# Gate columns and mLSTM values of a hybrid transformer block as one token-major product, done within the projections of another head group

## The chip, the cores and the metric

The kernel runs on one core of one Trainium2 chip. The metric is the device time of the whole program in microseconds (us): the median of three runs. All times are in us unless marked ns.

## The reference

Two layers work on 256 context tokens and 512 latent tokens of width 1024, in float32. Each layer norms and modulates the tokens, multiplies them with one input matrix whose columns belong to four groups of heads, joins what the groups give, multiplies with an output matrix, and then runs a gated MLP. Cut to what matters here:

```python
zx = split_cols(hx @ w_in)      # GDN q,k,v,z,a,b | SWA q,k,v | gMLP u,v | mLSTM q,k,v,o,i,f
a_x, a_c = gdn_mixer(...)       # bidirectional gated delta rule, chunks of 64 tokens
b_x, b_c = swa_mixer(...)       # windowed attention
c_x = gmlp_mixer(u, v, ...)     # u * (w_s @ rmsnorm(gelu(v)) + b_s), chunks of 128
d_x, d_c = mlstm_mixer(...)     # bidirectional mLSTM, chunks of 64
x = x + mod_x[2] * (concat(a, b, c, d) @ w_out)
x = x + mod_x[5] * mlp(...)
```

The gates of GDN (a, b) and of the mLSTM (i, f) are 16 columns each. They go through a softplus (GDN's decay and the mLSTM's forget gate); the mLSTM also needs a running maximum over all tokens.

## The kernel before, in words

Products run on TensorE in a split form: each float32 operand is split into a high part (ScalarE, `act_`, L182) and the rest (VectorE, L185 or L188), and three products are added: hi x hi, hi x lo, lo x hi (L179). The 768 tokens are one stretch of 256 (context) and one of 512 (latent); a projection of 128 columns (`gemm`) is 8 parts of the depth x 2 stretches x 3 products, 48 matmuls, with the weights stationary and the tokens streaming, and needs two PSUM buffers of the pool `pps` (four buffers, `ps()`). In the second layer some projections need the latent tokens alone. `gemm_pair` does two such projections in step, one part of the depth after the other, so that TensorE can begin while the norm's results `hhi` and `hlo` are still being made. `gemm_tok` does it the other way round: tokens stationary, 256 columns streaming, so that the result has tokens on its partitions; its results are called `mmt`, two blocks of 128 tokens to a PSUM buffer. `wload` loads 128 columns of weights (SP's queue, two buffers `wst`) and splits them into `whi` and `wlo`.

In one layer, `flow_kernel` goes in this order. (1) The pair behind the norm: the 32 gate columns, L620 and L632, and the first 128 columns of GDN's keys. The gates are copied out, transposed to tokens (`gatesT`, L636) and go through the softplus (L639 to L660), a chain of some 24 small VectorE operations that ends in `y` and `sp`. (2) The five other GDN projections, in the order v, k, v, q, q (L682 to L711), each followed by a convolution over tokens (four VectorE operations of 770 columns), a SiLU and, for k and q, a norm. (3) GDN's chunk work (L718 to L999): six steps of `gdn_pre`, `gdn_inv`, `gdn_kt` and `gdn_scan`, many small matmuls that wait for each other by way of VectorE and ScalarE. `N` is the first matrix of a chunk, `ops` the last matmuls of a step. Its tiles are in a pool `gd` that is closed at L1000 (`pa.close()`). (4) Projections of the other groups: attention (L1018 to L1030), the gMLP's values `vt` (L1058, `gemm_tok`) with their gelu (one buffer `tc`) and norm (L1067 to L1076), the mLSTM's keys and queries (L1087 to L1093), and the gMLP's mixing product `sg` (L1096 to L1110), the last reader of `vt`. (5) The mLSTM's gate scan (L1113 to L1198): cumulated sums `mb`, transposes `aRp`, the maximum scans (L1164) and what is made of them, `MD` last, in tiles of `tc`, `ta`, `tb` and a pool `sw1` opened behind `pa.close()` (`La`, `khi`). (6) The mLSTM's values, `va` (L1201 to L1204, `gemm_tok`, 144 matmuls). (7) A block `mix` (L1500 on) with attention, the mLSTM's chunks and the last projections woven together; its first matmuls are `decp`. Then come the output product and the MLP.

The order of the code is a priority: each engine gets the earliest instruction in the code that can go, so projections of stage (4) run in the gaps of stage (3). Buffers of one tag go to their users in the order of the code: `tc` has one, `ta` and `tb` two, the pool `pps` four, and `gi` and `go` one PSUM buffer each. The block `mix` begins only behind what stands before it on each engine.

Of the kernel before, what the change touches and what calls it, by code (L numbers as in the profile page):

```python
# [9 lines left out]
F32 = mybir.dt.float32  # L10
# [130 lines left out]
def flow_kernel(ctx, tc, t, out, dbg=None, stop=None):  # L141
# [20 lines left out]
    def ps(name="ps", dt=F32):  # L162
        return pps.tile([128, 512], dt, tag="ps", name=name)
# [20 lines left out]
    def tt(o, a, b, op, eng=None):  # L184
        (eng or V).tensor_tensor(out=o, in0=a, in1=b, op=op)  # L185
# [15 lines left out]
    def cc(name):  # L201
        o, w = _OFF[name]
        return cst[:, o:o + w]
# [75 lines left out]
    def evac(dst, o, segs, rows=128):  # L279
        for c0, cn in segs:  # L280
            act_(dst[:, c0:c0 + cn], o[bank(c0)][0:rows, 0:cn], AF.Copy)
# [196 lines left out]
    def wload(parts, order=None):  # L478
        st = wst.tile([128, 8, 128], F32, tag="wst", name="wst")
        o = 0  # L480
        for src in parts:
            n = src.shape[1]
            sv = src.rearrange("(k p) n -> p k n", p=128)
            for i in (range(0, 8, 2) if order else (0,)):
                if order:
                    nc.sync.dma_start(out=st[:, i:i + 2, o:o + n], in_=sv[:, order[i]:order[i] + 2])
                else:
                    nc.sync.dma_start(out=st[:, :, o:o + n], in_=sv)
            o += n
        return wsplit(st, o)  # L490
# [106 lines left out]
    for l in range(DEPTH):  # L597
# [19 lines left out]
        def z3(name, dt=F32):  # L617
            return zp.tile([128, NT], dt, tag="z3", name=name, bufs=6)

        ahead = [wload([win[:, C_AB:C_AB + 16], win[:, C_IF:C_IF + 16]]), wload([win[:, C_GK:C_GK + 128]])]  # L620
        h = modulated(l, 0, ALL, nrm, tp)
        del nrm
        xd = dp.tile([8, 128, NT], F32, tag="xd", name="xd")
# [3 lines left out]
        def temp(tag, w=GAP + 4):  # L627
            return tp.tile([128, GAP + 4], F32, tag=tag, name=tag, bufs=1 if tag == "tc" else 2)


        zg = temp("ta")
        o, o_k0 = gemm_pair(ahead, h, ALL, (32, 128))  # L632
        evac(zg[0:32], o, ALL, 32)
        o = ps("gatesT")
        for p in range(NP):
            T.transpose(o[:, 32 * p:32 * p + 32], zg[0:32, 128 * p:128 * p + 128], ident[0:32, 0:32])  # L636
        wb = z3("wb")
        ysp = z3("ysp")[:, 0:384].rearrange("p (x s g) -> p x s g", x=2, s=6)
        y, sp = ysp[:, 0], ysp[:, 1]  # L639
        u = temp("tb")[:, 0:192].rearrange("p (s g) -> p s g", g=32)  # L640
        w = temp("tc")[:, 0:192].rearrange("p (s g) -> p s g", g=32)
        tt(y, o[:, 0:192].rearrange("p (s g) -> p s g", g=32), bc(tokp[l][:, 0:32], 1, 6), ADD)
        tt(y, y, bc(cc("sgn"), 1, 6), MUL)
        nega = tokp[l][:, 32:40]
        act_(nega, nega, AF.Exp)
        V.tensor_scalar(out=nega, in0=nega, scalar1=-1.0, scalar2=None, op0=MUL)

        V.tensor_scalar(out=sp, in0=y, scalar1=-1.0, scalar2=None, op0=MUL)
        tt(u, sp, y, MAX)
        act_(u, u, AF.Exp, scale=-1.0)  # L650
        V.tensor_scalar(out=w, in0=u, scalar1=2.0, scalar2=None, op0=ADD)
        V.reciprocal(out=w, in_=w)
        tt(u, u, w, MUL)
        tt(w, u, u, MUL)
        V.tensor_scalar(out=sp, in0=w, scalar1=1.0 / 15, scalar2=None, op0=MUL)
        for cf in (13, 11, 9, 7, 5, 3):
            stt(sp, sp, 1.0 / cf, w, ADD, MUL)
        stt(sp, sp, 1.0, u, ADD, MUL)
        V.tensor_scalar(out=u, in0=y, scalar1=0.0, scalar2=None, op0=MAX)
        stt(sp, sp, 2.0, u, MUL, ADD)  # L660


        kq = [gd.tile([128, 2, GAP], F32, name=f"kq{j}") for j in range(2)]
# [16 lines left out]
                stt(x[:, a0:], x[:, a0:], f, e[:, a0:], MUL, MUL)  # L680

        cols = [(C_GK, C_GQ, C_GV)[which] + 128 * j for which, j in ((0, 0), (2, 0), (0, 1), (2, 1), (1, 0), (1, 1))]  # L682
        ready = {}
        for i, (which, j) in enumerate(((0, 0), (2, 0), (0, 1), (2, 1), (1, 0), (1, 1))):
            qlat = which == 1 and last
            segs = LAT if qlat else ALL
            o = gemm(None, h, segs, w2=ready.pop(i)) if i else o_k0
            if i < 5:
                ready[i + 1] = wload([win[:, cols[i + 1]:cols[i + 1] + 128]])
            raw = temp("ta")  # L690
            G.memset(raw[:, 0:2], 0.0)
            G.memset(raw[:, 258:260], 0.0)
            G.memset(raw[:, 772:774], 0.0)
            if not qlat:
                act_(raw[:, 2:258], o[0][:, 0:256], AF.Copy)
            act_(raw[:, 260:772], o[1], AF.Copy)
            a0 = 258 if qlat else 0
            acc = vf[j] if which == 2 else kq[j][:, which]
            cw = R_CONV + {0: 2, 1: 0, 2: 4}[which] + j
            act_(acc[:, a0:], raw[:, a0:GAP], AF.Copy, scale=prm[l][:, cw:cw + 1])  # L700
            for tp_ in range(1, 5):
                stt(acc[:, a0:], raw[:, a0 + tp_:GAP + tp_], prm[l][:, cw + 6 * tp_:cw + 6 * tp_ + 1], acc[:, a0:], MUL, ADD)
            e = temp("tb")[:, 0:GAP] if i % 2 else gd.tile([128, 1024], F32, tag="at", name="e", bufs=2)[:, 0:GAP]
            sigmoid_(acc[:, a0:], e[:, a0:])
            tt(acc[:, a0:], acc[:, a0:], e[:, a0:], MUL)
            if len(unit) > 2 - 1:
                unit_rows()
            if which < 2:
                act_(e[:, a0:], acc[:, a0:], AF.Square)
                unit.append((acc, e, a0, 0.125 if which else None))  # L710
# [344 lines left out]
            act_(w_, w_, AF.Exp, scale=-1.0)  # L1055
            tt(x, x, w_, MUL)

        vt = zp.tile([128, 6, 264], F32, tag="big", name="vt")[:, :, 0:256]  # L1058
        gemm_tok(l, C_MV, opairs, h, lambda p, o: act_(vt[:, p], o, AF.Copy))
        for p0, pn in ((0, 4), (4, 2)):  # L1060
            o = ps("svT")
# [34 lines left out]
        for j in range(2):  # L1096
            for p0 in range(opairs[0], NP, 4):
                pn = min(4, NP - p0)
                o = ps("sg")
                for p in range(p0, p0 + pn):  # L1100
                    for g in (2 * j, 2 * j + 1):
                        gp_ = slice(64 * (g % 2), 64 * (g % 2) + 64)
                        mm(o[gp_, 128 * (p - p0):128 * (p - p0) + 128], vt[:, p, 64 * g:64 * g + 64], wsT[:, g, :])
                n_ = 128 * pn
                mv = mix[4 + j][:, 128 * p0:128 * p0 + n_]
                sgt = temp("ta")[:, 0:n_] if early else mv
                stt(sgt.rearrange("p (a b) -> p a b", b=128), o[:, 0:n_].rearrange("p (a b) -> p a b", b=128),
                    prm[l][:, R_GMW + j:R_GMW + j + 1], bc(bsb[:, j], 1, pn), MUL, ADD)
                if early:
                    tt(mv, mv, sgt, MUL)  # L1110


        pb = ctx.enter_context(ExitStack())  # L1113
# [81 lines left out]
        for p in range(NP):  # L1195
            mm(o[:, 64 * p:64 * p + 64], bc(mlast[:, p], 1, 128), ident[0:64, 0:64])
        tt(ks, am, o[:, 0:384].rearrange("p (a d r) -> p a d r", a=6, d=2)[:, :, :, 0:4], SUB)
        act_(ks, ks, AF.Exp)  # L1198


        va = zp.tile([128, 6, 4, 66], F32, tag="big", name="va")  # L1201
        G.memset(va[:, :, :, 64:66], 1.0)
        gemm_tok(l, C_LV, list(range(NP)), h,
                 lambda p, o: act_(va[:, p, :, 0:64], o.rearrange("p (h i) -> p h i", h=4), AF.Copy))  # L1204

        if stop == "A":
            return
# [416 lines left out]
```

## Time and profile before

| | us |
|---|---|
| median of 3 runs | 1977.71 |
| lowest and highest run | 1973.69, 1981.29 |
| profiled execution, its own time | 1960.3 |
| its span, first to last instruction | 1958.5 |
| TensorE busy, share of the span | 96% |
| VectorE busy, share of the span | 61% |
| ScalarE busy, share of the span | 39% |
| mean granted TensorE clock | 0.979 |

The profile is of one execution. PE is TensorE, DVE is VectorE, ACT is ScalarE, POOL is GpSimd, SP issues most loads. Matmuls are pipelined, so the time from one to the next is shorter than one's duration. A row "out<-in" names the tile written and the tiles read; a bracket at the end of a row gives how long the engine had been idle before and what let it go.

### The profile page before, as it was taken

The page shows a single profiled execution, that of the slowest core. Times are in us where ns is not written, and L with a number is a line of the kernel's source. Part 1 is how long each engine was busy: PE and PEld are TensorE (multiplying, and loading weights), DVE is VectorE, ACT ScalarE, POOL GpSimd, SP SyncE. Part 2 cuts the span into 40 slices and gives each one's busy share as a digit, 9 for nine tenths or more (in the row PEclk, how much of TensorE's full clock was granted, in tenths as well). Part 3 has the DMA queues.
Part 4 walks back from the last instruction along what each step waited for, and adds up shares of the span by engine and source line. Part 5 has one row for each costly group of instructions (what it writes and reads, how often), then busy time and mean ns, then how long its engine had stood idle before and what let it go on. Part 6 is the DMA issues. An engine that isn't in the chain of part 4 may idle for free.

```text
span 1958.5 us, 33935 instructions
## 1 busy us (share of the span) xinstructions
PE 1881.4 (96%) x14107; PEld 1539.8 (79%) x14107; DVE 1196.3 (61%) x2210; ACT 754.2 (39%) x1528; POOL 101.1 (5%) x163
## 2 busy tenths in 40 slices
PE   6999999999899999999999999999999999999998
PEld 3877778778777888888888878677777778888887
DVE  3878875666659566435535349788777754444443
ACT  4652234455424312312213236534355543333242
POOL 0021210000000000000000000212100000000001
PEclk8999989999799999999999999999999999999999
DMA  9220001111364345335423222201011323333332
GB/s 324 80 52 24 23 13 44 57 55 44 120 203 128 109 140 147 94 116 151 129 84 122 81 62 54 63 23 34 23 44 33 102 76 103 97 97 97 97 97 76
DMA packets 225634, 172.28 MB, mean 88 GB/s; under 512 B 19042, under 2 KB 207816, under 8 KB 225480
## 3 DMA queue, kind: packets, MB, share of 16 engines
q1 hardware_dynamic: 219104, 153.38, 26.5%
q10 hardware_dynamic: 4680, 10.70, 1.5%
q0 software_dynamic: 1696, 6.03, 0.9%
q8 instruction: 110, 1.80, 0.4%
q14 instruction: 44, 0.36, 0.1%
HBM read 162.75 MB, written 7.34 MB: 87 GB/s over the span
## 4 chain that ended last, share of the span: by engine, by line
PE 82%; DVE 10%; ACT 4%; DMA 3%; issue 1%; POOL 0%; DVEq 0%; ACTq 0%; SPq 0%; POOLq 0%
PE mm L179 63%; PE mmt L179 2%; PE num L179 1%; PE ops L179 1%; DVE kq L188 1%; DMA wst<-w_in 1%; PE pv L179 1%; DVE wlo L185 1%; PE yt L179 1%; DVE Y L185 1%; PE adaps L179 1%; PE pT L1340 1%; PE t L179 1%; PE Eps L179 1%; PE yps L179 1%
## 5 line engine op out<-in xcount | busy, mean ns | idle before, releaser
L182 ACT ACTIVATE whi<-wst 128x512 fp32r<-128x512 f32 (+1 forms) x388 | 241.7, 627 | 682.2 <-PE mm L179 623.5
L179 PE MATMUL mm<-hhi,whi 128*128 128x512 f32 (+3 forms) x1344 | 477.8, 361 | 12.8 <-ACT hhi L182 11.4
L179 PE MATMUL mm<-hlo,whi 128*128 128x512 f32 (+3 forms) x1344 | 479.4, 357 | 1.5 <-DVE hlo L188 1.3
L179 PE MATMUL mm<-hhi,wlo 128*128 128x512 f32 (+3 forms) x1344 | 475.3, 356 | 0.1
L185 DVE TENSOR_TENSOR wlo<-wst,whi 128x512 fp32r<-128x512 f32 (+1 forms) x388 | 265.1, 687 | 313.3 <-ACT whi L182 309.4
L179 PEld LDWEIGHTS mm<-hhi,whi 128*128 128x128 f32 (+1 forms) x1344 | 251.9, 188 | 55.4 <-ACT hhi L182 14.9
L179 PEld LDWEIGHTS mm<-hlo,whi 128*128 128x128 f32 (+1 forms) x1344 | 253.1, 188 | 39.9 <-DVE hlo L188 3.6
L179 PEld LDWEIGHTS mm<-hhi,wlo 128*128 128x128 f32 (+1 forms) x1344 | 252.2, 188 | 39.0 <-issue 2.8
L179 PE MATMUL mm<-fhi,whi 128*128 128x512 f32 (+1 forms) x784 | 276.0, 352 | 0.0
L179 PE MATMUL mm<-flo,whi 128*128 128x512 f32 (+1 forms) x784 | 276.0, 352 | 0.0
L179 PE MATMUL mm<-fhi,wlo 128*128 128x512 f32 (+1 forms) x784 | 274.6, 350 | 0.0
L188 DVE SCALAR_TENSOR_TENSOR x<-mm,mod,x 128x256 f32<-128x256 f32 (+1 forms) x122 | 79.7, 653 | 142.4 <-PE mm L179 142.3
L179 PEld LDWEIGHTS mm<-fhi,whi 128*128 128x128 f32 x784 | 148.4, 189 | 21.7 <-ACT whi L182 0.8
L179 PEld LDWEIGHTS mm<-fhi,wlo 128*128 128x128 f32 x784 | 148.1, 189 | 19.7
L179 PEld LDWEIGHTS mm<-flo,whi 128*128 128x128 f32 x784 | 148.4, 189 | 19.2
L188 DVE SCALAR_TENSOR_TENSOR adacc<-adw,scT,adacc 128x1024 f32<-128x1024 f32 x84 | 105.8, 1281 | 28.3 <-DMA adw<-ada_w 28.2
L185 DVE TENSOR_TENSOR flo<-r,fhi 128x768 fp32r<-128x768 f32 (+1 forms) x64 | 52.6, 824 | 39.2 <-ACT fhi L182 39.1
L182 ACT ACTIVATE fhi<-r 128x768 fp32r<-128x768 f32 (+1 forms) x64 | 47.2, 740 | 66.8 <-DVE r L185 66.8
L179 PE MATMUL mm<-mlo,whi 128*128 128x512 f32 (+1 forms) x192 | 71.0, 370 | 1.3 <-DVE mlo L185 1.3
L179 PE MATMUL mm<-mhi,whi 128*128 128x512 f32 (+1 forms) x192 | 70.6, 368 | 0.4 <-ACT mhi L182 0.4
L179 PE MATMUL mm<-mhi,wlo 128*128 128x512 f32 (+1 forms) x192 | 70.0, 365 | 0.0
L182 ACT ACTIVATE r<-mm 128x256 f32<-128x256 f32 (+1 forms) x96 | 49.1, 514 | 31.5 <-PE mm L179 31.5
(404 smaller groups left out, 2712.3 us busy)
## 6 DMA issues: line engine op xcount, KB each, us to landing
wst<-mlp_w SPq DMA_DIRECT2D x128, 512.0 KB, 4.0
adw<-ada_w SPq DMA_DIRECT2D x96, 512.0 KB, 4.3
wst<-w_in SPq DMA_DIRECT2D x44, 512.0 KB, 3.7
wst<-w_out SPq DMA_DIRECT2D x64, 128.0 KB, 3.1
xd<-x ACTq DMA_DIRECT2D x8, 384.0 KB, 3.5
x<-xd POOLq DMA_DIRECT2D x8, 384.0 KB, 5.2
xs<-x ACTq DMA_DIRECT2D x4, 512.0 KB, 6.9
wst<-w_in SPq DMA_DIRECT2D x8, 256.0 KB, 3.4
```

Source lines behind the costliest of these rows:

```text
L179: T.matmul(o, lhsT=l, rhs=r, start=start, stop=stop)
L182: S.activation(out=o, in_=i, func=f, **kw)
L185: (eng or V).tensor_tensor(out=o, in0=a, in1=b, op=op)
L188: V.scalar_tensor_tensor(out=o, in0=a, scalar=s, in1=b, op0=op0, op1=op1)
L1340: T.transpose(o[:, 256 * i + 128 * g:256 * i + 128 * g + 128], Ps[g][:, 128 * (i0 + i):128 * (i0 + i) + 128], ident)
```

## The change

The gates leave the pair behind the norm, and the first 128 value columns of GDN take their place. The 32 gate columns are joined to the 256 value columns of the mLSTM as one block of 288 columns with the tokens stationary: weights come in four chunks of 256 rows, each by three loads (256, 16 and 16 columns), are split into tiles of the tag `z3`, and six PSUM buffers (four of `ps`, `gi` and `go`) take the six blocks of 128 tokens. The block is called behind the fifth GDN projection (the first of q), ahead of that projection's copy out of PSUM; the softplus follows it. The product of the mLSTM's values at its old place goes, and `va` is made at the start of the layer in the place of the tag `big`. `vt`, which shared that place, gets a pool of its own, opened behind `pa.close()` and closed ahead of the pool that holds `sw1`.

```diff
-        ahead = [wload([win[:, C_AB:C_AB + 16], win[:, C_IF:C_IF + 16]]), wload([win[:, C_GK:C_GK + 128]])]
+        ahead = [wload([win[:, c:c + 128]]) for c in (C_GK, C_GV)]
...
-        zg = temp("ta")
-        o, o_k0 = gemm_pair(ahead, h, ALL, (32, 128))
-        evac(zg[0:32], o, ALL, 32)
-        o = ps("gatesT")
-        for p in range(NP):
-            T.transpose(o[:, 32 * p:32 * p + 32], zg[0:32, 128 * p:128 * p + 128], ident[0:32, 0:32])
...
+        va = zp.tile([128, 6, 4, 66], F32, tag="big", name="va")
+
+        def gates():
+            G.memset(va[:, :, :, 64:66], 1.0)
+            o = [ps("mmt"), ps("mmt"), gi("mmt"), go1("mmt"), ps("mmt"), ps("mmt")]
+            for kk in range(0, 8, 2):
+                st = wst.tile([128, 8, 128], F32, tag="wst", name="wst").rearrange("p k n -> p (k n)")[:, 0:576]
+                st = st.rearrange("p (k n) -> p k n", k=2)
+                for n0, c0, cn in ((0, C_LV, 256), (256, C_AB, 16), (272, C_IF, 16)):
+                    nc.sync.dma_start(out=st[:, :, n0:n0 + cn], in_=win[128 * kk:128 * kk + 256, c0:c0 + cn]
+                                      .rearrange("(k p) n -> p k n", p=128))
+                hi, lo = (z3(x, F32R)[:, 0:576].rearrange("p (k n) -> p k n", k=2) for x in ("ghi", "glo"))
+                act_(hi, st, AF.Copy)
+                tt(lo, st, hi.bitcast(F32), SUB)
+                for p in range(NP):
+                    for k in range(2):
+                        ahi, alo = h[kk + k]
+                        for pi, (w_, a) in enumerate(((hi, ahi), (hi, alo), (lo, ahi))):
+                            mm(o[p][:, 0:288], a[:, 128 * p:128 * p + 128], w_[:, k],
+                               start=(kk == k == pi == 0), stop=(kk + k == 7 and pi == 2))
+            for p in range(NP):
+                act_(va[:, p, :, 0:64], o[p][:, 0:256].rearrange("p (h i) -> p h i", h=4), AF.Copy)
+                tt(y[:, p], o[p][:, 256:288], tokp[l][:, 0:32], ADD)
...
-        ready = {}
+        first = gemm_pair(ahead, h, ALL, (128, 128))
+        ready = {2: wload([win[:, cols[2]:cols[2] + 128]])}
         for i, (which, j) in enumerate(((0, 0), (2, 0), (0, 1), (2, 1), (1, 0), (1, 1))):
             qlat = which == 1 and last
             segs = LAT if qlat else ALL
-            o = gemm(None, h, segs, w2=ready.pop(i)) if i else o_k0
-            if i < 5:
+            o = first[i] if i < 2 else gemm(None, h, segs, w2=ready.pop(i))
+            if 0 < i < 5:
                 ready[i + 1] = wload([win[:, cols[i + 1]:cols[i + 1] + 128]])
+            if i == 4:
+                gates()
             raw = temp("ta")
...
-        vt = zp.tile([128, 6, 264], F32, tag="big", name="vt")[:, :, 0:256]
+        pv_ = ctx.enter_context(ExitStack())
+        vt = pv_.enter_context(tc.tile_pool(name="vt", bufs=1)).tile([128, 6, 256], F32, name="vt")
...
+        pv_.close()
...
-        va = zp.tile([128, 6, 4, 66], F32, tag="big", name="va")
-        G.memset(va[:, :, :, 64:66], 1.0)
-        gemm_tok(l, C_LV, list(range(NP)), h,
-                 lambda p, o: act_(va[:, p, :, 0:64], o.rearrange("p (h i) -> p h i", h=4), AF.Copy))
```

The softplus between the two parts of `gates()` is the one of before, word for word. In the text, GQ0 and GQ1 are the two projections of GDN's queries.

## Rows read from the trace of the kernel before

**Rows 1.** The page, busy time and share of the span by engine, with instructions.
```profile
PE 1881.4 (96%) x14107; PEld 1539.8 (79%) x14107; DVE 1196.3 (61%) x2210; ACT 754.2 (39%) x1528; POOL 101.1 (5%) x163
```
**Rows 2.** Busy time by stage of layer 0: stretch, length, engines, PEclk, DMA, GB/s.
```profile
62.00:108.00 46.00, 45.70 (x261) 39.03 (x260) 38.03 (x69) 28.10 (x45) 1.30 (x18) 1.00 0.22 58
...
246.00:309.50 63.50, 61.27 (x962) 47.76 (x961) 47.00 (x101) 25.56 (x67) 6.79 (x8) 0.92 0.07 19
309.50:328.00 18.50, 18.50 (x106) 15.97 (x105) 4.34 (x9) 7.77 (x13) 1.42 (x2) 1.00 0.20 58
```
**Rows 3.** The chain of waits that ended last: start, us, what, with count.
```profile
309.53 18.53 PE mm L179 x103
328.06 2.77 PE sg L179 x48
...
345.69 9.92 PE mmt L179 x81
...
683.69 66.25 PE mm L179 x378
...
1424.31 8.95 PE mmt L179 x73
```
**Rows 4.** Instructions in order of time, ends of the scan, both layers: start, us, engine, instruction.
```profile
347.11 1.01 DVE L188 SCALAR_TENSOR_TENSOR MD<-rhi,cst,ta 64x768 fp32r<-64x768 f32 x1
...
355.52 0.39 PE L179 MATMUL decp<-MD,sel_r 32*128 32x6 f32 x4
...
1415.83 1.01 DVE L188 SCALAR_TENSOR_TENSOR La<-rhi,cst,ta 64x768 fp32r<-64x768 f32 x1 [0.98 <-ACT rhi L182]
...
1425.73 1.01 DVE L188 SCALAR_TENSOR_TENSOR MD<-rhi,cst,ta 64x768 fp32r<-64x768 f32 x1
...
1433.17 0.39 PE L179 MATMUL decp<-MD,sel_r 32*128 32x6 f32 x4
```
**Rows 5.** Instructions in order of time, POOL at the end of GDN, both layers.
```profile
309.75 0.73 POOL L1147 MEMSET La<- 64x768 f32 x1 [3.71 <-PE ops L179]
...
1411.54 0.74 POOL L1147 MEMSET La<- 64x768 f32 x1 [6.64 <-PE ops L179]
```
**Rows 6.** Groups by shape, TensorE, 44 to 64 us: count, busy us, mean ns, idle before.
```profile
L179 PE MATMUL mm<-hhi,whi 128*32 128x512 f32 x8 | 3.6, 453 | 0.2 <-ACT hhi L182 0.2
L179 PE MATMUL mm<-hhi,whi 128*128 128x512 f32 x8 | 3.6, 452 | 0.0
```
**Rows 7.** Last query projection in order of time, both layers; a convolution group by shape.
```profile
110.26 0.58 ACT L182 ACTIVATE ta<-mm 128x512 f32<-128x512 f32 x1
...
132.92 0.68 DVE L185 TENSOR_TENSOR N<-gq,N 128x512 f32<-128x512 f32 x1
...
1224.51 0.58 ACT L182 ACTIVATE ta<-mm 128x512 f32<-128x512 f32 x1
...
1241.18 0.68 DVE L185 TENSOR_TENSOR N<-gq,N 128x512 f32<-128x512 f32 x1
...
L188 DVE SCALAR_TENSOR_TENSOR kq<-ta,prm,kq 128x770 f32<-128x770 f32 x12 | 12.1, 1010 | 3.2 <-ACT kq L182 3.1
```
**Rows 8.** Loads: issues by kind, count, KB each, median us from issue to landing.
```profile
wst<-w_in SPq DMA_DIRECT2D x44, 512.0 KB, 3.7
...
wst<-w_in SPq DMA_DIRECT2D x4, 64.0 KB, 6.1
```
**Rows 9.** Instructions in order of time, the gMLP's values in layer 0.
```profile
245.04 0.66 ACT L182 ACTIVATE vt<-mmt 128x256 f32<-128x256 f32 x2 [1.85 <-PE mmt L179]
...
300.21 0.63 ACT L182 ACTIVATE tc<-vt 128x512 f32<-128x512 f32 x1 [0.76 <-DVE vt L185]
...
304.55 0.69 DVE L185 TENSOR_TENSOR vt<-vt,tc 128x512 f32<-128x512 f32 x1 [0.61 <-ACT tc L182]
...
306.91 1.66 DVE L1076 TENSOR_SCALAR vt<-vt,gss 128x256 f32<-128x256 f32 x6
```
**Rows 10.** Busy time by stretch, the start of the mixing block in layer 0.
```profile
356.00:366.00 10.00, 6.39 (x32) 3.97 (x33) 4.85 (x17) 6.46 (x17) 0.00 (x0) 0.66 0.12 27
```

More of the change, by code (lines that the diff above doesn't have):

```diff
@@ L639, in flow_kernel @@
         y, sp = ysp[:, 0], ysp[:, 1]
[L640 to L659, printed above, removed]
@@ L660, in flow_kernel @@
-        stt(sp, sp, 2.0, u, MUL, ADD)
+        va = zp.tile([128, 6, 4, 66], F32, tag="big", name="va")
[20 more added lines that the diff above has]
+                tt(y[:, p], o[p][:, 256:288], tokp[l][:, 0:32], ADD)
+            u = temp("tb")[:, 0:192].rearrange("p (s g) -> p s g", g=32)
+            w = temp("tc")[:, 0:192].rearrange("p (s g) -> p s g", g=32)
+            tt(y, y, bc(cc("sgn"), 1, 6), MUL)
+            nega = tokp[l][:, 32:40]
+            act_(nega, nega, AF.Exp)
+            V.tensor_scalar(out=nega, in0=nega, scalar1=-1.0, scalar2=None, op0=MUL)
+            V.tensor_scalar(out=sp, in0=y, scalar1=-1.0, scalar2=None, op0=MUL)
+            tt(u, sp, y, MAX)
+            act_(u, u, AF.Exp, scale=-1.0)
+            V.tensor_scalar(out=w, in0=u, scalar1=2.0, scalar2=None, op0=ADD)
+            V.reciprocal(out=w, in_=w)
+            tt(u, u, w, MUL)
+            tt(w, u, u, MUL)
+            V.tensor_scalar(out=sp, in0=w, scalar1=1.0 / 15, scalar2=None, op0=MUL)
+            for cf in (13, 11, 9, 7, 5, 3):
+                stt(sp, sp, 1.0 / cf, w, ADD, MUL)
+            stt(sp, sp, 1.0, u, ADD, MUL)
+            V.tensor_scalar(out=u, in0=y, scalar1=0.0, scalar2=None, op0=MAX)
+            stt(sp, sp, 2.0, u, MUL, ADD)
```

## The prediction, made before the result was known

> **What bounds the kernel now.** I read the page first. TensorE is busy for 96% of the span [rows 1], so at first sight every matmul that goes is time. The second view, busy time by stage of layer 0, is there to test that. In the projections (62 to 108 us) TensorE is full and VectorE is busy for 38 of 46 us; in the GDN chunks (246 to 309.5) both have gaps; from 309.5 to 328 TensorE is full and the others nearly idle [rows 2]. The reader is to see three regimes: projections bound by TensorE with VectorE close behind, a GDN chain of dependent small steps whose gaps are filled by projections of later groups ("fillers"), and a tail of fillers left over when GDN has ended. The third view, the chain of waits, shows the tail: 103 filler matmuls in 18.53 us, the 48 sg matmuls, and, behind the scan of the mLSTM gates, the last 81 (layer 1: 73) matmuls of the mLSTM values in 9.92 and 8.95 us [rows 3]. The fourth view, instructions in order of time, shows what stands behind them: MD, the scan's last result, is there at 348.1, but decp, TensorE's first work in the mixing block, starts at 355.52; in layer 1, where La is written from 1415.83 on, the two are 1426.7 and 1433.17 [rows 4]. There the values' projection ends last. The fifth view is the end of GDN: the memset of La starts at 309.75 and 1411.54, let go by the last ops matmuls of GDN, though it reads nothing of GDN and POOL had stood idle for 3.7 and 6.6 us [rows 5]. La is a tile of a pool that is opened behind pa.close(): such a pool gets its place only when all of GDN's tiles are done with.
>
> **The change, part by part.**
>
> Removed: the gates' own product, 24 matmuls of 256 and 24 of 512 columns. With 32 output columns a matmul takes as long as with 128 (453 and 452 ns) [rows 6], so it costs a full projection: 48 x 66.25/378 = 8.4 us a layer [rows 3]. The six small transposes that go with it I leave out of the sum. The values' projection at its old place, 144 matmuls at 9.92/81 = 0.122 us, 17.6 us, goes as well.
>
> Added: 144 matmuls of 288 columns. No row has 288. At 256 columns it is 0.122 us; 256 and 512 together take 2 x 0.175, so 512 is 0.228, and in between 0.136 us: 19.5 us in all (bounds 17.6 and 144 x 0.228 = 32.8; I take 19.5, as 288 is near 256). TensorE's work falls by 8.4 + 17.6 - 19.5 = 6.5 us a layer.
>
> Pair behind the norm: keys and values of GDN in place of gates and keys, again 96 matmuls of the same lengths, waiting for the same hhi and hlo. Two more splits of 128x512 weights stand in front of it on ScalarE and VectorE, where the loads of 64-byte rows stood. I cost it at nothing (bounds -1 and +1): the activations are late either way.
>
> Moved ahead, where the GDN projections are: behind the pair come three projections, the joined block, and GQ1, where there were five projections. GQ1 ends 19.5 - 8.4 = 11.1 us later on TensorE. From GQ1's evacuation to N, the first chunk matrix, it took 110.26 to 132.92 in layer 0 and 1224.51 to 1241.18 in layer 1 [rows 7]. Its own operations are about 16, the four longest at 1.01 us, some 13 us in layer 0: the other 9 are VectorE working off earlier convolutions. The joined block gives VectorE 19.5 us with only four splits in them, so it catches up, but then the softplus chain, which used to be spread over the first projections, stands in GQ1's way, with priority over it. So GDN begins between 0 and 11.1 us later; I take +3 in layer 0 and +5 in layer 1, where the chain had less waiting in it (16.7 us) to give back.
>
> On SP's queue one load of two pieces becomes twelve issues in four chunks, all ahead of the block. A chunk keeps TensorE busy for 4.9 us and two are in flight, so I cost them at nothing; the cover is GQ0's projection. A load of gate columns (64 KB) took 6.1 us to land, one of 512 KB 3.7 [rows 8]. The Trainium skill, "DMA: Bandwidth & Descriptors", section "Specifications", wants 512 bytes or more in a piece for full rate; the trace agrees, and by that rule alone the gate columns, now cut up further but still 64 bytes to a row, would be what a chunk waits for (rival 4, 1999 us).
>
> Moved behind: vt, the gMLP values, goes from the layer's pool to a pool opened behind pa.close(). Like La, it can be written only when GDN has ended. Before, vt left PSUM from 245 us on, and the gelu chain and the scaling ran inside GDN's time, done by 308.6 [rows 9]. Now six evacuations (0.66 us for two, 2.0 us), three gelu passes one after the other through the one tc buffer (300.21 to 305.24, 5.0 us each), and 3.3 us of squares and scaling come behind: 20.3 us in layer 0, 1.4 + 10.0 + 2.7 = 14.1 in layer 1, which has four blocks of tokens. Until then three (layer 1: two) of the four PSUM buffers of the fillers are held. Queued behind on the single tc buffer are ab and M of the gate scan; La's pool, opened when vt's is closed, waits for vt's last reader, sg.
>
> Layer 0: GDN ends +3. The fillers left then are 18.5 us, plus about 4 that lost their time ahead of GDN (between 0 and 11.1 - 3), plus 2 for the held PSUM (0 to 15): 24.5. That covers the 20.3 us of vt, so sg ends 3 + 4 + 2 = 9 us later. From sg's end (330.83) to decp were 24.7 us; now decp follows MD, and the last 81 of the values' matmuls, 9.92 us, with the others that stood between the scan's transposes, are gone: -8.5, since La's memset now waits for sg (bounds -11 and -6). Sum +0.5.
>
> Layer 1: its fillers ended before GDN, so nothing covers vt. From the end of GDN (1411.5) to decp it was 21.6 us. Now: 14.1 us of vt, sg's 32 matmuls (2.77 x 32/48 = 1.8) and the start of their evacuation until La can be written at 16.2, then La to MD as before, 10.9 [rows 4], and 1 for the clock: 28.1, or +6.5 (bounds -6.4, if vt is not held and only the values' tail behind MD goes, and +12). With GDN's +5: +11.5. The clock: in a stretch where TensorE was busy for 6.4 of 10 us its granted clock was 0.66 [rows 10], between its two levels of 1.2 and 2.4 GHz; at the lower level sg's 1.8 us would be 3.7, and I take half. The Trainium skill, "TensorE: Matmul & The Clock Gate", section "Why this matters for your kernels", warns of idle gaps between bursts for this reason; the row agrees.
>
> Sum: 0.5 + 11.5 = +12 us. The profiled execution took 1960.3 us (span 1958.5), below all three timed runs (median 1977.7); so 1972 on its scale, and 1990 on the median's, from which all times below are counted.
>
> **The rivals.**
> 1. *The hold does not bite, and GDN starts on time.* If vt gets its place while GDN runs, layer 1 saves the values' tail (-6.4) and layer 0 gains 4 - 8.5 = -4.5: -11, 1967 us, faster. It decides at one point: vt's first evacuation before GDN's last ops. For it: TensorE has 2 x 6.5 = 13 us less to do. Against: [rows 5], in both layers.
> 2. *The hold does not bite, but GDN starts late*: +3 and +5 on top of that, -3 in all, 1975 us, no change.
> 3. *The fillers starve.* Three of four PSUM buffers held could stop the mLSTM key and query projections until GDN ends: 192 matmuls, 33.6 us instead of 22.5 behind it, so 11 more: 2001 us. Against: a projection can go through one buffer, half by half.
> 4. *The chunks come late.* If each waits for its gate columns, 6.1 against 4.9 us, four times in two layers: +9.6, 1999 us.
> That the change does not do what it says would show in the count of 288-column matmuls; I see no way to it.
>
> **How the numbers follow.** Forecast 0.45, of which 0.16 falls within 0.5% (its terms reach from -6 to +25 us), rival 1 0.18, rival 2 0.20, rival 3 0.12, rival 4 0.05. Half a per cent, 10 us, is about what a measurement of this kernel can tell from no change. Slower: 0.29 + 0.12 + 0.05 = 0.46; same: 0.16 + 0.20 = 0.36; faster 0.18. The range, 1966 to 2006, takes in rivals 2 to 4 and reaches to rival 1; as signs are mixed, the forecast's own range is 1980 to 2002.
>
> **What would show it.** Right: vt<-mmt begins just behind GDN's last ops in both layers; in layer 1 TensorE has a hole of some 15 us there, with a low clock, and aRp comes behind the second gelu; decp follows MD within a microsecond; N comes 2 to 6 us later. Wrong: vt evacuated while GDN runs, mb and aRp at GDN's end, TensorE waiting for wst in the block, or a tail of fillers behind GDN in layer 0 far from 25 us.

## The result and the profile after

The changed kernel takes 2003.53 us (median of 5 runs, 1996.93 to 2007.24), the kernel before in the same comparison 1973.69 (1967.29 to 1981.29): ratio 1.0153, 95% interval 1.0114 to 1.0193. It is about 30 us, or 1.5%, slower. The profiled execution after took 2003.5 us (span 2001.8), its median. The profiled execution before, 1960.3 us, was faster than all runs of its kernel here, so the difference of the two spans, 43.3 us, is more than the change costs; a second profile of the unchanged kernel (b2_before_again, below, span 1972.7) sets that right.

Instructions in order of time, the changed kernel: GDN's first chunk matrix, GDN's end, the scan's end, in both layers.

```profile
123.49 0.58 ACT L182 ACTIVATE ta<-mm 128x512 f32<-128x512 f32 x1
...
145.57 0.69 DVE L185 TENSOR_TENSOR N<-gq,N 128x512 f32<-128x512 f32 x1 [0.80 <-PE gq L179]
...
326.45 0.66 PE L179 MATMUL ops<-ATb,yy 128*64 128x128 f32 x8 [0.53 <-ACT yy L182]
...
367.36 0.73 POOL L1171 MEMSET La<- 64x768 f32 x1 [19.15 <-PE sg L179]
...
381.59 1.01 DVE L188 SCALAR_TENSOR_TENSOR MD<-rhi,cst,ta 64x768 fp32r<-64x768 f32 x1
...
382.75 0.59 PE L179 MATMUL decp<-MD,sel_r 32*128 32x6 f32 x4 [1.43 <-DVE MD L188]
...
1261.11 0.58 ACT L182 ACTIVATE ta<-mm 128x512 f32<-128x512 f32 x1
...
1282.73 0.69 DVE L185 TENSOR_TENSOR N<-gq,N 128x512 f32<-128x512 f32 x1 [3.66 <-POOL N L185]
...
1447.68 1.21 ACT L182 ACTIVATE vt<-mmt 128x256 f32<-128x256 f32 x4 [0.29 <-PE ops L179]
...
1476.19 1.01 DVE L188 SCALAR_TENSOR_TENSOR MD<-rhi,cst,ta 64x768 fp32r<-64x768 f32 x1
...
1477.35 0.59 PE L179 MATMUL decp<-MD,sel_r 32*128 32x6 f32 x4 [1.43 <-DVE MD L188]
```

These answer to [rows 4, 5, 7]. The hold (vt gets its memory only when GDN is done with it) bites in both layers: vt's evacuations, the copies out of PSUM, come right behind GDN's last ops. decp now follows MD at once. The chain of waits in layer 0 (start, us, what, with count) shows the joined block in one piece and what stands behind GDN:

```profile
95.61 19.20 PE mmt L179 x144
...
327.30 1.77 ACT vt L182 x6
329.11 35.25 PE mm L179 x192
364.37 2.79 PE sg L179 x48
```

192 filler matmuls in 35.25 us stand where 103 in 18.53 stood [rows 3]: all four of the mLSTM's key and query projections. The same chain in layer 1, where vt's own chain ends last: two passes of the gelu through its single buffer tc, then ab in the same buffer, sg, and only then the rest of the scan.

```profile
1447.68 1.21 ACT vt L182 x4
...
1457.65 0.70 DVE vt L185
1458.36 0.05 issue
1458.41 0.75 POOL tc L1150
...
1461.12 1.93 PE sg L179 x32
1463.08 0.84 ACT khi L182
...
1471.38 1.97 PE Mt L179 x8
1473.35 2.57 PE Ml L179 x12
```

TensorE is not idle beside the gelu in layer 1. 48 matmuls of projections, which before were all done ahead of GDN's end, stand behind it now. Busy time in that stretch, columns as in [rows 2]:

```profile
1447.50:1457.20 9.70, 9.70 (x51) 8.27 (x50) 4.68 (x11) 7.69 (x19) 0.00 (x0) 1.00 0.20 56
```

The steps of the three profiles, in us (each is the difference of two rows like those above; "sg" is its first matmul):

| step | before | before again | after | predicted, after - before | after - before | after - before again |
|---|---|---|---|---|---|---|
| to the first hhi | 43.9 | 46.6 | 47.4 | 0 | +3.5 | +0.8 |
| layer 0: hhi to N | 89.1 | 88.2 | 98.2 | +3 | +9.1 | +10.0 |
| N to last ops | 176.6 | 173.9 | 181.5 | 0 | +4.9 | +7.6 |
| last ops to sg | 18.5 | 18.5 | 37.2 | +6 | +18.7 | +18.7 |
| sg to decp | 27.5 | 31.9 | 18.4 | -8.5 | -9.1 | -13.5 |
| decp to layer 1's hhi | 810.0 | 811.5 | 808.5 | 0 | -1.5 | -3.0 |
| layer 1: hhi to N | 75.6 | 76.6 | 91.5 | +5 | +15.9 | +14.9 |
| N to last ops | 170.1 | 173.9 | 164.8 | 0 | -5.3 | -9.1 |
| last ops to decp | 21.8 | 26.3 | 29.8 | +6.5 | +8.0 | +3.5 |
| decp to the end | 525.4 | 525.3 | 524.4 | 0 | -1.0 | -0.9 |
| span | 1958.5 | 1972.7 | 2001.8 | +12 | +43.3 | +29.1 |

Against the second profile the steps add up to 29.1 us, what the medians say. Layer 0 loses 19.9 of it: 10.0 before N, 7.6 within GDN, and 5.2 from GDN's end to decp, where a gain of 2.5 was forecast; 3.0 come back later. Layer 1 loses 14.9 before N and 3.5 behind GDN and wins 9.1 within it.

### The profile page after: what moved, and what is told of

It is laid out like the page before. It is cut to its first block, busy times and chain, and to the rows that moved or that the text cites. A ratio compares the mean times of both kernels' runs of the same rounds, so it can differ in the third digit from the quotient of the medians.

```text
span 2001.8 us, 33759 instructions
## 1 busy us (share of the span) xinstructions
PE 1891.9 (95%) x13999; PEld 1557.0 (78%) x13999; DVE 1205.8 (60%) x2220; ACT 757.4 (38%) x1524; POOL 99.7 (5%) x163
## 4 chain that ended last, share of the span: by engine, by line
PE 82%; DVE 9%; ACT 3%; DMA 3%; issue 1%; POOL 1%; ACTq 0%; DVEq 0%; POOLq 0%
PE mm L179 62%; PE mmt L179 3%; PE ops L179 1%; PE num L179 1%; DVE Y L185 1%; PE adaps L179 1%; PE pv L179 1%; PE yt L179 1%; PE t L179 1%; PE Eps L179 1%; PE pT L1358 1%; PE scl L179 1%; PE yps L179 1%; DMA adw<-ada_w 1%; DVE hy L188 1%
## 5 line engine op out<-in xcount | busy, mean ns | idle before, releaser
L182 ACT ACTIVATE whi<-wst 128x512 fp32r<-128x512 f32 x380 | 238.1, 631 | 642.6 <-PE mm L179 596.6
L179 PE MATMUL mm<-hhi,whi 128*128 128x512 f32 (+1 forms) x1312 | 467.7, 361 | 11.4 <-ACT hhi L182 10.2
L179 PE MATMUL mm<-hlo,whi 128*128 128x512 f32 (+1 forms) x1312 | 470.6, 359 | 1.2 <-DVE hlo L188 0.9
L179 PE MATMUL mm<-hhi,wlo 128*128 128x512 f32 (+1 forms) x1312 | 466.4, 357 | 0.5 <-DVE wlo L185 0.5
L185 DVE TENSOR_TENSOR wlo<-wst,whi 128x512 fp32r<-128x512 f32 x380 | 259.8, 689 | 308.7 <-ACT whi L182 305.5
L179 PEld LDWEIGHTS mm<-hhi,whi 128*128 128x128 f32 x1312 | 251.0, 192 | 51.1 <-ACT hhi L182 13.2
L179 PEld LDWEIGHTS mm<-hlo,whi 128*128 128x128 f32 x1312 | 252.1, 192 | 38.1 <-DVE hlo L188 3.3
L179 PEld LDWEIGHTS mm<-hhi,wlo 128*128 128x128 f32 x1312 | 251.6, 192 | 36.7 <-issue 1.7
L179 PEld LDWEIGHTS mm<-fhi,whi 128*128 128x128 f32 x784 | 148.3, 189 | 21.8 <-ACT r L182 0.8
L182 ACT ACTIVATE r<-mm 128x256 f32<-128x256 f32 (+1 forms) x96 | 49.1, 515 | 31.9 <-PE mm L179 31.9
```

The source lines that it names most:

```text
L179: T.matmul(o, lhsT=l, rhs=r, start=start, stop=stop)
L182: S.activation(out=o, in_=i, func=f, **kw)
```

## Experiments

All kernels compute the whole reference. Ratios are to the kernel before. The theory at the start: vt's hold on PSUM leaves the fillers behind GDN in layer 0 (rival 3 of the prediction, there), and GDN's late start is the rest.

**The hold alone.** The kernel before with this edit only:

```diff
-        vt = zp.tile([128, 6, 264], F32, tag="big", name="vt")[:, :, 0:256]
+        pv_ = ctx.enter_context(ExitStack())
+        vt = pv_.enter_context(tc.tile_pool(name="vt", bufs=1)).tile([128, 6, 256], F32, name="vt")
...
+        pv_.close()
         pb = ctx.enter_context(ExitStack())
```

> The kernel before with one edit: vt gets its pool behind the end of GDN, as in the change; gates, values and pair stay as they were. Theory (the hold is most of the loss in layer 0: vt's three PSUM buffers are held, and a projection needs two at once): the six vt evacuations come within 1 us of GDN's last ops matmul in both layers; in layer 0 all four projections of the mLSTM's keys and queries, 192 matmuls, stand behind GDN, some 35 us in place of 18.5; layer 0's decp 10 to 17 us after where it was against GDN's end, layer 1's 6 to 12; first chunk matrix N unmoved within 1.5 us of the layer's first hhi; the whole 15 to 28 us slower than before (ratio 1.008 to 1.014). Rival (the loss is GDN's late start, the hold is covered): within 6 us of before (ratio 0.997 to 1.003), tail in layer 0 103 to 120 matmuls.

Measured: 2001.54 us, ratio 1.0155 (1.0119 to 1.0190), as much as the whole change and a little above the 15 to 28 us expected. N is unmoved. Its chain of waits, both layers:

```profile
307.85 0.67 ACT vt L182 x2
310.10 34.76 PE mm L179 x192
344.86 2.79 PE sg L179 x48
357.37 1.15 PE mmt L179 x4
362.98 13.51 PE mmt L179 x94
...
1437.38 1.21 ACT vt L182 x4
...
1449.60 3.59 PE sg L179 x32
1462.93 1.93 PE mmt L179 x9
1469.32 12.49 PE mmt L179 x87
```

The 192 matmuls are there. GDN's end to decp is 68.7 and 44.5 us, 22.7 more than in the first profile of before in each layer and 18 more than in the second, beyond both expectations. In the changed kernel the two are 55.6 and 29.8; here the values' product still follows behind MD (13.51 and 12.49 us), which makes most of the difference. The change takes that tail away: of what the hold costs, it gives part back.

**No hold.** The changed kernel with vt in the two tiles that later take sg's results; all sg matmuls go before the first result is written:

```diff
-        pv_ = ctx.enter_context(ExitStack())
-        vt = pv_.enter_context(tc.tile_pool(name="vt", bufs=1)).tile([128, 6, 256], F32, name="vt")
+        mix[4], mix[5] = (xm.tile([128, NT], F32, tag="xm", name="uu") for j in range(2))
+        def vts(p, n):
+            j, a = (0, p - 2) if p in (2, 3) else (1, p - 4) if p > 3 else (p, 2)
+            return mix[4 + j][:, 256 * a:256 * (a + n)]
```

> The changed kernel with vt in the places that the gMLP's two result tiles take anyway (the sg matmuls all go before the first result is written), so that it needs nothing of GDN's memory. Theory: vt leaves PSUM while GDN runs; layer 0 tail 90 to 125 matmuls in place of 192, GDN end to decp some 37 us in place of 55.6; layer 1, GDN end to decp 14 to 17 us in place of 29.8; N as late as in the changed kernel (within 2 us of it, counted from the layer's first hhi). The whole 18 to 32 us faster than the changed kernel, so about the time of before: ratio to before 0.998 to 1.007. Rival (the late start is the whole loss): within 6 us of the changed kernel, ratio to before 1.012 or more.

Measured: 1982.96 us, ratio 1.0052 (1.0033 to 1.0071). The chain of waits behind GDN in layer 0, and the busy time of two stretches of the scan (columns as in [rows 2]), one in each layer:

```profile
327.19 18.76 PE mm L179 x104
345.94 2.36 PE sg L179 x40
```

```profile
348.70:365.50 16.80, 8.21 (x50) 7.23 (x48) 13.66 (x36) 3.01 (x5) 2.09 (x3) 0.65 0.00 1
...
1440.80:1457.00 16.20, 8.16 (x48) 7.18 (x48) 13.10 (x34) 3.53 (x6) 2.09 (x3) 0.66 0.00 0
```

The fillers are back in GDN's time; the hold costs the changed kernel 20 us, of which 17.2 lie between GDN's end and decp in layer 0 and 7.2 in layer 1, less 4.2 by which layer 1's GDN was shorter with it. Layer 1 missed its expectation: GDN's end to decp is 22.7 us, not 14 to 17, with a few projection matmuls still to do behind GDN (4.35 us in 18). And without the hold the change is still no gain. Against the second profile of before N is 10.6 and 16.1 us late (98.8 and 92.7 us from the first hhi), and GDN's end to decp only 12.0 and 3.6 shorter: during the scan TensorE is busy for half the time at a granted clock of 0.65, as the product that used to fill the scan is gone.

**Order of the fillers.** The changed kernel with vt's product, gelu and scaling behind the mLSTM's projections in the code:

```diff
-        pv_ = ctx.enter_context(ExitStack())
-        vt = pv_.enter_context(tc.tile_pool(name="vt", bufs=1)).tile([128, 6, 256], F32, name="vt")
-        gemm_tok(l, C_MV, opairs, h, lambda p, o: act_(vt[:, p], o, AF.Copy))
...
         lq = mix[6:8]
+        pv_ = ctx.enter_context(ExitStack())
+        vt = pv_.enter_context(tc.tile_pool(name="vt", bufs=1)).tile([128, 6, 256], F32, name="vt")
+        gemm_tok(l, C_MV, opairs, h, lambda p, o: act_(vt[:, p], o, AF.Copy))
+        for p in range(opairs[0], NP, 2):
+            gelu(vt[:, p:p + 2], 512)
...
```

> The changed kernel, still with the hold, but the product for vt, its gelu and scaling stand in the code behind the mLSTM's key and query projections. Theory (the tail of 192 matmuls in layer 0 comes from the PSUM buffers that vt holds): the four projections go back into GDN's time, and behind GDN stand at most some 60 filler matmuls; vt's chain of 24 us then ends last, so sg begins some 25 us behind GDN in layer 0 in place of 37, and layer 0 is 8 to 14 us shorter than in the changed kernel; layer 1 within 4 us of it. Rival (the projections are late for another reason, the one tc buffer or the weights): they stay behind GDN, sg 35 us or more behind it.

Measured: 2005.03 us, ratio 1.0169 (1.0138 to 1.0200). In layer 0 the four projections go back into GDN's time and not one of their matmuls stands behind it, which bears out the theory on PSUM; the layer is 12.1 us shorter (1131.8 against 1143.9, hhi to hhi). But 139 of vt's own 144 matmuls are then behind GDN, more than the 60 expected, and sg begins 31.0 us behind it, not 25. Layer 1, where the old order had room, becomes 12.8 us longer: the second expectation failed, and the whole is unchanged.

**The block two projections earlier**, to see what N waits for:

```diff
-            if i == 4:
+            if i == 2:
                 gates()
```

> The changed kernel with the joined block two projections earlier (behind the first product after the pair, in place of behind the first query product). Theory: in layer 0 N hangs on the last query projection, 22 us from its evacuation, and that does not move: N within 1.5 us of the changed kernel, counted from the first hhi; in layer 1 N hangs on the softplus and the decays behind it, so N comes 3 to 6 us earlier. Whole: 2 to 7 us faster than the changed kernel. Rival (VectorE's backlog ahead of GDN sets N, as the prediction had it, and the softplus moved forward lets it catch up): N 6 us or more earlier in both layers.

Measured: 2004.37 us, ratio 1.0165 (1.0132 to 1.0198), the same as the changed kernel. From the last query projection's evacuation to N it is 22.6 us in layer 0 and 16.2 in layer 1 (changed kernel 22.1 and 21.6), so in layer 1 the softplus and the decays behind it had cost 5 us; but that projection itself is evacuated 3 us later in both layers, which eats most of it. N comes 3.4 us later in layer 0, 2.2 earlier in layer 1, short of the 3 to 6 expected there. The rival, a backlog of VectorE that would clear and bring N 6 us forward in both layers, did not show.

**Values last.** No hold, and the projections in the order keys, queries, values:

```diff
-        for i, (which, j) in enumerate(((0, 0), (2, 0), (0, 1), (2, 1), (1, 0), (1, 1))):
+        for i, (which, j) in enumerate(((0, 0), (0, 1), (1, 0), (1, 1), (2, 0), (2, 1))):
```

> The kernel without the hold (e2_no_hold) with another order of the GDN projections: keys, keys, queries, queries, values, values; the pair behind the norm is then the two key products, and the joined block stands behind the first value product. Theory: N is set in layer 0 by the 22 us from the last query projection's evacuation (convolution, SiLU, two norms in line), not by a backlog of VectorE; values have no norm, so with them last N hangs on the decays instead: N 5 to 9 us earlier in layer 0 (counted from the first hhi), 0 to 3 us in layer 1; whole 4 to 10 us faster than e2_no_hold, ratio to before 1.000 to 1.004. Rival (VectorE is simply full until then): N within 2 us of e2_no_hold in both layers.

Measured: 1972.14 us, ratio 1.0013 (0.9991 to 1.0035), within the theory's range. The last projection's evacuation to N shrinks from 22.1 to 16.4 us in layer 0 and from 22.2 to 12.8 in layer 1, but that projection comes 3.6 and 6.4 us later, so N gains only 2.0 and 3.0, where 5 to 9 and 0 to 3 were expected. Of the two statements on N this settles neither; the view of that stretch in the next section says more.

**The scan ahead of the projections.** If the scan's hole is what the change leaves behind, the projections left behind GDN should fill it:

```diff
+        pb = ctx.enter_context(ExitStack())
+        sw1 = pb.enter_context(tc.tile_pool(name="sw1", bufs=1))
+        o = gi("mb")
...
+        act_(ks, ks, AF.Exp)
         lk = [z3("lk") for j in range(2)]
...
+        for dst, c0, sg2 in ((lk[0], C_LK, ALL), (mix[6], C_LQ, osegs), (mix[7], C_LQ + 128, osegs), (lk[1], C_LK + 128, ALL)):
```

> The kernel without the hold (e2_no_hold) with the mLSTM's gate scan moved in the code ahead of its key and query projections, so that sg and the projections left behind GDN run beside it (the last key projection last of the four, since MD now takes the tile that it had). Theory: with the values' product gone from behind GDN nothing fills the scan's gaps, TensorE is idle 8 us there in each layer, and that is why the change without the hold gains nothing. GDN end to decp 22 to 27 us in layer 0 in place of 38.4, 15 to 19 in layer 1 in place of 22.7; whole 14 to 22 us faster than e2_no_hold, ratio to before 0.994 to 0.999. Rival (the scan's time is not what ends last there, decp waits for the projections anyway): within 4 us of e2_no_hold.

Measured: 1968.54 us, ratio 0.9985 (0.9964 to 1.0005), 14 us under the kernel without the hold, and not clearly apart from the kernel before. Busy time behind GDN, both layers:

```profile
321.00:349.00 28.00, 26.99 (x196) 23.02 (x195) 18.21 (x47) 12.60 (x26) 4.54 (x5) 1.00 0.13 40
1422.80:1440.00 17.20, 13.48 (x86) 12.11 (x88) 12.91 (x29) 10.19 (x20) 2.82 (x4) 0.80 0.00 0
```

TensorE is full in layer 0's stretch, at full clock, and GDN's end to decp is 28.2 us in place of 38.4 (22 to 27 expected), in layer 1 17.5 in place of 22.7. The same move in the kernel before, together with the edit of e2_no_hold for vt:

> The same move of the scan in the kernel before (gates first, values' product at its old place behind the scan in the code; vt in the places of the gMLP's result tiles as in e2_no_hold, so that va has the old place for itself). Theory: here the values' product, 144 matmuls or 17.6 us, still has to run behind GDN in layer 0, so GDN end to decp is 36 to 43 us in place of 46.0 and in layer 1 16 to 24 in place of 21.8; whole 2 to 12 us faster than before, ratio 0.994 to 0.999. Rival (the scan alone is worth it, and the change adds nothing): ratio within 0.002 of e6_scan_ahead's.

Measured: 1977.67 us, ratio 1.0032 (1.0007 to 1.0056): no gain, slightly slower. Its chain of waits behind sg:

```profile
333.28 17.47 PE mmt L179 x144
...
1431.34 17.48 PE mmt L179 x144
```

The whole values' product comes behind the scan now, 17.5 us in each layer with nothing beside it. Layer 0 stays at 45.7 us from GDN's end to decp and layer 1 grows to 35.1, against the 36 to 43 and 16 to 24 expected. So the scan's move, with vt's new place, is worth nothing in the kernel before; with the block it is worth some 14 us.

**Both moves together**, the edits of e5_values_last and e6_scan_ahead:

> e5_values_last and e6_scan_ahead together: the joined block with no hold, values last, scan ahead. Theory: the two gains lie in different stretches and add up: ratio to before 0.988 to 0.996, N as in e5_values_last, GDN end to decp as in e6_scan_ahead. Rival (an earlier GDN only lengthens the tail of projections behind it): no faster than e6_scan_ahead within 3 us.

Measured: 1973.47 us, ratio 1.0008 (0.9985 to 1.0030). The gains don't add: in layer 0 N is 2.6 us earlier than in e6_scan_ahead, but GDN takes 182.4 us from N in place of 177.0 and its end to decp 34.0 in place of 28.2. Why is open.

**By layer.** Layer 0 as in e6_scan_ahead, layer 1 as in the kernel before (every edit under a test on `l`):

```diff
+        if l == 0:
             ahead = [wload([win[:, c:c + 128]]) for c in (C_GK, C_GV)]
+        else:
+            ahead = [wload([win[:, C_AB:C_AB + 16], win[:, C_IF:C_IF + 16]]), wload([win[:, C_GK:C_GK + 128]])]
...
+        for part in ("scan", "proj", "sg") if l == 0 else ("proj", "sg", "scan"):
```

> Layer 0 as in e6_scan_ahead (joined block, no hold, scan ahead of the projections), layer 1 as in the kernel before. Theory: in layer 0 projections are left over when GDN ends, so TensorE's time is what counts and 6.5 us less work shows there; in layer 1 they all fit in GDN's time, so what is put ahead of GDN is lost. So layer 0, from its first hhi to layer 1's, is 1113 to 1119 us (before 1121.7, e6 1116.0) and layer 1 to the end 791 to 796 (before 793.0, e6 802.8); whole 4 to 12 us faster than before, ratio 0.994 to 0.998. Rival (layer 0's gain in e6_scan_ahead was the profiled run's chance, or it is the scan and not the block): ratio 0.999 or more.

Measured: 1959.76 us (1956.79 to 1965.50, 12 runs), before 1970.76; ratio 0.9953 (0.9934 to 0.9973). This one beats both kernels. Layer 0 takes 1117.1 us, as expected, under the 1121.7 and 1124.0 of the two profiles of before and the 1120.9 of e7_before_scan_ahead, which has all but the block; layer 1 takes 797.2, a little over the 791 to 796. That speaks for the block in layer 0, where projections are left over behind GDN. That it loses in layer 1, where they all fit in GDN's time, fits the medians of this run and of e6_scan_ahead (layer 1 there 802.8) but is not shown: the two profiles of before differ by more in that layer (793.0 and 802.1).

**The gates alone in the block**, values back at their old place, no hold:

```diff
-                for n0, c0, cn in ((0, C_LV, 256), (256, C_AB, 16), (272, C_IF, 16)):
+                for n0, c0, cn in ((0, C_AB, 16), (16, C_IF, 16)):
...
-                            mm(o[p][:, 0:288], a[:, 128 * p:128 * p + 128], w_[:, k],
+                            mm(o[p][:, 0:32], a[:, 128 * p:128 * p + 128], w_[:, k],
```

> The kernel without the hold (e2_no_hold) with a block of the 32 gate columns alone at the same place, and the mLSTM's values back at their old place behind the scan. It separates the length of the block ahead of GDN from where the softplus stands. Theory: the block is some 8 us, about what the gates cost before, so the last query projection is evacuated 64 to 69 us after the first hhi in layer 0 and 57 to 62 in layer 1, as before (66.4 and 59.0); but the softplus and the decays still come behind it, so in layer 1 from there to N it stays 19 to 22 us (before 16.7), in layer 0 22 to 24. Rival (the block's length alone makes GDN late): 16 to 18 us there in layer 1, and N as before.

Measured: 2027.84 us, ratio 1.0275 (1.0227 to 1.0324). The block did not shrink to 8 us. Its line in the chain of waits, and its busy time in two stretches, with the granted clock third from the end:

```profile
94.31 25.95 PE mmt L179 x144
```

```profile
94.31:99.00 4.69, 4.69 (x45) 4.69 (x44) 2.39 (x4) 3.26 (x6) 0.00 (x0) 1.00 0.50 122
99.50:120.20 20.70, 20.70 (x99) 20.70 (x98) 3.66 (x9) 2.54 (x3) 0.00 (x0) 0.50 0.17 39
```

and the block of the changed kernel:

```profile
95.61:114.81 19.20, 19.20 (x146) 19.20 (x146) 8.66 (x15) 9.77 (x15) 0.00 (x0) 1.00 0.35 85
```

With 32 columns the granted clock fell to its lower level within the block; layer 1's took 28.20 us. So the block's length was not taken away: the last query projection is evacuated 84.3 and 82.5 us after the first hhi, not 64 to 69 and 57 to 62, and this run can't say what GDN would do without the block. What it does show is the softplus: in layer 1 the last query projection to N is 20.0 us, as the theory had it (19 to 22), against 16.7 before.

**The two kernels again:**

> The kernel before, unchanged, profiled once more. If the steps are the program's own, then hhi to N, last ops to sg and the others repeat within 1.5 us, and N to the last ops (176.6 in layer 0, 170.1 in layer 1) within 2 us. Rival (differences of 5 us in GDN's length are the execution's chance): N to last ops moves by 3 us or more.

> The changed kernel, unchanged, profiled once more. If the steps are the program's own: hhi to N 98.2 and 91.5, N to last ops 181.5 and 164.8, last ops to decp 55.6 and 29.8, each within 2 us, and the first hhi 3 us later than in the kernel before. Rival (chance of the execution): N to last ops moves by 3 us or more.

Measured: 1974.48 and 2004.21 us. The changed kernel repeats every step within 2 us (N to last ops 182.6 and 164.8). Its first hhi comes at 45.9 this time, before the 46.6 of the second profile of before: the later start was chance. The kernel before does not repeat: N to last ops moves by -2.7 and +3.8, and the ends of its scans by +4.4 in both layers. Chain of waits and busy time of the second profile of before, behind the scan in layer 0:

```profile
342.75 1.90 PE Mt L179 x8
344.65 2.56 PE Ml L179 x12
347.21 11.96 PE mmt L179 x81
```

```profile
336.00:359.00 23.00, 21.54 (x139) 20.92 (x137) 13.60 (x26) 4.88 (x11) 1.18 (x2) 0.78 0.08 24
```

The same 81 matmuls took 9.92 us in the first [rows 3]; here the granted clock of the stretch is 0.78, in the first 0.98. The first profile had both scans at full clock (1.00 between 331.0 and 348.2 us and between 1416 and 1427; in the second 0.80 and 0.69 in the like stretches), and that is where most of its 14 us of luck lies, 8.8 of 14.2.

## Why the prediction was right, and where it was wrong

The time lies in the range (1966 to 2006) and on the side forecast as likelier than the others, slower. The mechanism that it named, vt held until GDN ends, is shown: alone it costs 31 us, and without it the changed kernel is 20 us faster. The size, +12 for some 30, is wrong in two terms, GDN's late start and the fillers behind it. Part of the hit is luck: the time is above the forecast's own range (1980 to 2002) and next to the 2001 us of rival 3, which had 0.12. The two terms were too low by 29.6 us together against the second profile, and the whole by only 17, as other steps came out shorter than forecast. Of its signs, vt just behind the last ops, aRp behind the second gelu and decp behind MD came true; the hole in TensorE's time in layer 1 and N's 2 to 6 us did not.

- *The joined block*, 19.5 us: 19.20 measured, 0.133 us a matmul for 0.136. Right. *The pair behind the norm* at nothing: right; the first hhi moves by chance in both kernels. *The chunks* at nothing: right; the 144 matmuls follow each other without a wait for wst, and the loads of gate columns land sooner than those before (6.1 us, [rows 8]):

```profile
wst<-w_in SPq DMA_DIRECT2D x16, 16.0 KB, 2.5
```

  The Trainium skill, "DMA: Bandwidth & Descriptors", section "Specifications", stood behind rival 4; whatever rate those short rows had, it did not come to bear here.
- *"So GDN begins between 0 and 11.1 us later; I take +3 ... and +5."* This failed. The last query projection came 9.7 and 10.9 us later, as worked out. But from there to N it took 22.1 and 21.6 us, for 22.7 and 16.7 before, so that N was 9.1 and 15.9 us late. The working took 9 of the 22.7 us for VectorE's backlog, which the block would let it clear. The stretch from that projection to N, before and after, shows no backlog to clear, as VectorE was busy for 14.7 and 14.6 us of it (third of the busy times) and TensorE for nearly all:

```profile
110.26:132.92 22.66, 21.93 (x149) 16.20 (x149) 14.74 (x30) 18.27 (x37) 6.25 (x8) 1.00 0.33 86
```

```profile
123.49:145.57 22.08, 21.13 (x148) 15.95 (x147) 14.55 (x40) 15.07 (x31) 6.41 (x8) 1.00 0.31 78
```

  The projection's own chain of convolution, SiLU and norm fits that: with a projection without a norm last, the stretch was 16.4 us (e5_values_last). In layer 1 the bound of 11.1 was itself too low: it left out the decays, which also wait for the softplus (e4_gates_early, e12_gates_only). The granted clock was 0.68 in that stretch for 1.00 before; how much of the 5 us it made is open.
- *"The fillers left then are 18.5 us, plus about 4 ..., plus 2 for the held PSUM."* This failed: 37.2 us, and rival 3 is what happened in layer 0 (in layer 1 the 48 matmuls left behind GDN ran beside vt's chain and cost little). The sentence against it, "a projection can go through one buffer, half by half", is wrong: gemm's two stretches keep one buffer each through the whole product. Nor was one buffer left. In layer 0 of the changed kernel the rotation's product (rope) sat in the fourth:

```profile
195.28 1.02 PE L179 MATMUL rope<-sq,cst 128*128 128x512 f32 x2
...
328.01 0.99 PE L1085 MATMUL svT<-cst,tc 128*128 128x128 f32 x6 [0.90 <-ACT vt L182]
...
329.31 0.68 DVE L185 TENSOR_TENSOR tc<-rope,tb 128x512 f32<-128x512 f32 x1
```

  It waited 133 us for the tc buffer, which held the attention values until their transposes (svT) found a PSUM buffer, and those stood behind vt's three. So no filler ran in the last 44 us of GDN.

```profile
283.40:327.10 43.70, 32.62 (x574) 27.29 (x571) 27.69 (x61) 8.74 (x19) 4.29 (x5) 0.69 0.05 14
```

- *From sg to decp in layer 0*, -8.5: -9.1 measured, against the second profile -13.5. Right in kind. *From GDN's end to decp in layer 1*, 28.1 us: 29.8. Right: 18.2 us to La for the 16.2 worked out, 11.7 from there to decp for 11.9; vt, the gelu and ab run one behind the other in tc. Its premise that no fillers were left was wrong. The half-speed term, 1 us, was put at sg; the clock fell at Mt and Ml instead (1.97 and 2.57 us at a granted clock of 0.50 between 1469.9 and 1476 us; before 1.10 and 1.34 at 1.00).
- *The scale.* The sum was made on an execution 13 us below its median and carried over as a constant. That most of the median's extra time lay at the ends of the scans, where the values' tail stood that the change removes, could not be seen in one profile.

Still open: GDN's own length, N to last ops in layer 0, which lies anywhere from 172.6 to 182.6 us in these profiles, whichever way the edits went.

## What to carry to other kernels

When a tile moves to memory that is free only later, ask what holds its source: here the products stayed in three of four PSUM buffers, a rotation's product that waited in a ring for the same pool kept the fourth, and every projection behind them starved. Work taken out of a stretch bound by latency leaves a hole, and work put ahead of a chain that nothing covers delays all of it; here the block paid only once the scan ran beside the projections left over. Profile the kernel before twice before a sum is made of single microseconds.

## What was not expected of the hardware

TensorE's granted clock fell while it was busy without a gap. In e12_gates_only's block of 32 streaming columns, each matmul behind a weight load of 128 columns, a matmul began every 0.11 us at a granted clock of 1.00, and about 5 us into the block the clock fell to 0.50, the lower of its levels, 1.2 GHz; from there one began every 0.21 us to the block's end. With 288 columns all 144 ran at 1.00, one in 0.133 us, and with 256 in 0.122. So at full clock the short matmuls were the cheapest by a little, and the clock made their block the longest. Why it fell there no run shows.

GDN's length did not follow the granted clock: between 283.4 and 327.1 us it was 0.69 in the changed kernel and 0.96 without the hold,

```profile
283.40:327.10 43.70, 41.69 (x644) 31.86 (x644) 35.02 (x77) 20.45 (x47) 3.87 (x4) 0.96 0.10 26
```

yet layer 0's GDN took 181.5 and 181.7 us from N. This does not show that the clock costs nothing: the faster stretch also had 70 more matmuls in it, as fillers ran there.
